# Rotary embedding in f32: one in-order SP queue of 2 MB transfers, and six of 32 tiles summed on TensorE

## The chip, the core and the metric

The kernel runs on one core of a Trainium2 chip. The engines that matter: VectorE (DVE in the profile), GpSimd (POOL), ScalarE (ACT), TensorE (PE), and SyncE (SP), which computes nothing and issues DMA transfers. The transfers of every queue are carried out by the same 16 DMA engines of the core. The metric is device time in microseconds of the slowest (here the only) core, lower is better.

## The reference: what is computed

```python
x1 = x[..., : x.shape[-1] // 2]
x2 = x[..., x.shape[-1] // 2 :]
cos = cos[None, :, None, :]
sin = sin[None, :, None, :]
out1 = x1 * cos - x2 * sin
out2 = x1 * sin + x2 * cos
return np.concatenate([out1, out2], axis=-1)
```

`x` is 8 x 2048 x 8 x 64 in f32 (batch, position, head, feature), 33.55 MB; `cos` and `sin` are 2048 x 32, 0.26 MB each. The output has the shape of `x`. So every byte of `x` is read once and written once, and each element takes part in two multiplications and one addition.

## The kernel before

The 2048 positions are spread over 128 partitions, 16 consecutive positions (R) per partition. A row of one partition and one batch is therefore 16 x 512 f32, 32 KB, contiguous in memory. The kernel cuts it into four pieces of four positions (SL = 4): a tile is 128 partitions x 2048 elements, 1 MB, and there are 32 tiles, ordered by piece and then by batch.

- **Loads** (L55) go through the SP queue, all 32 in a loop ahead of the computation. The pool `xpool` has 20 buffers, so loads from the 21st on wait for a store to release a buffer.
- **Tables**: sine and cosine are loaded through the ACT queue (L48, L49). VectorE writes a negated and a plain copy of the sine side by side into `ssin` (L58, L59), and copies the cosine to PSUM (L60).
- **Per tile**: GpSimd multiplies the swapped halves by the signed sine into `t2`, one instruction per half (L73, two per tile; `t2_pool` has three buffers). VectorE multiplies the tile by the cosine into `t1`, which lies in PSUM (L78, one buffer), and adds `t1` and `t2` back into the tile (L83). The tile is stored through the ACT queue (L84).

Each engine works through its own stream in order. VectorE alternates L78 and L83 of one tile after the other; GpSimd may be ahead of it by as many tiles as `t2` has buffers. ScalarE does no arithmetic, its queue issues the two table loads and the 32 stores; TensorE is not used. In the tables of the profile `t` stands for the `t1` and `t2` buffers.

Of the kernel before, what the change touches and what calls it, by code (L numbers as in the profile page):

```python
# [2 lines left out]

# [4 lines left out]


@with_exitstack  # L10
def kernel(
    ctx: ExitStack,
    tc: tile.TileContext,
    x: bass.AP,
    cos: bass.AP,
    sin: bass.AP,
    out: bass.AP,
):
    nc = tc.nc
    f32 = mybir.dt.float32  # L20

    B, S, H, D = x.shape
    Dh = D // 2
    P = 128
    HD = H * D
    R = S // P

    SL = 4
    n_blk = R // SL
    FREE = SL * HD  # L30

    xv = x.rearrange("b (q r) h d -> b q (r h d)", q=P)
    ov = out.rearrange("b (q r) h d -> b q (r h d)", q=P)
    cos_src = cos.rearrange("(q r) d -> q r d", q=P)
    sin_src = sin.rearrange("(q r) d -> q r d", q=P)

    const_pool = ctx.enter_context(tc.tile_pool(name="const", bufs=1))
    cps_pool = ctx.enter_context(tc.tile_pool(name="cps", bufs=1, space=bass.MemoryType.PSUM))
    t1_pool = ctx.enter_context(tc.tile_pool(name="t1p", bufs=1, space=bass.MemoryType.PSUM))
    xpool = ctx.enter_context(tc.tile_pool(name="xpool", bufs=20))  # L40
    t2_pool = ctx.enter_context(tc.tile_pool(name="t2p", bufs=3))

    cos_sb = const_pool.tile([P, R, Dh], f32, tag="cb")
    sin_sb = const_pool.tile([P, R, Dh], f32, tag="sb")
    ssin = const_pool.tile([P, R, 2, Dh], f32, tag="ss")
    cos_ps = cps_pool.tile([P, R, Dh], f32, tag="cp")

    nc.scalar.dma_start(out=sin_sb, in_=sin_src)  # L48
    nc.scalar.dma_start(out=cos_sb, in_=cos_src)  # L49

    tiles = [(b, l) for l in range(n_blk) for b in range(B)]
    xts = []
    for i, (b, l) in enumerate(tiles):
        xt = xpool.tile([P, FREE], f32, tag="xt", name=f"xt{i}")
        nc.sync.dma_start(out=xt, in_=xv[b, :, l * FREE : (l + 1) * FREE])  # L55
        xts.append(xt)

    nc.vector.tensor_scalar_mul(ssin[:, :, 0, :], sin_sb, -1.0)  # L58
    nc.vector.tensor_copy(ssin[:, :, 1, :], sin_sb)  # L59
    nc.vector.tensor_copy(cos_ps, cos_sb)  # L60

    def rep(a, n):
        return dataclasses.replace(a, ap=[a.ap[0][:], a.ap[1][:], [0, n], a.ap[-1][:]])

    for i, (b, l) in enumerate(tiles):
        xt = xts[i]
        t1 = t1_pool.tile([P, FREE], f32, tag="t1")
        t2 = t2_pool.tile([P, FREE], f32, tag="t2")

        for u in range(2):  # L70
            dst = t2.rearrange("p (rh u d) -> p rh u d", u=2, d=Dh)[:, :, u, :]
            src = xt.rearrange("p (rh u d) -> p rh u d", u=2, d=Dh)[:, :, 1 - u, :]
            nc.gpsimd.tensor_mul(  # L73
                out=dst.rearrange("p (r h) d -> p r h d", h=H),
                in0=src.rearrange("p (r h) d -> p r h d", h=H),
                in1=rep(ssin[:, l * SL : (l + 1) * SL, u, :], H),
            )
        nc.vector.tensor_mul(  # L78
            out=t1.rearrange("p (r k d) -> p r k d", r=SL, d=Dh),
            in0=xt.rearrange("p (r k d) -> p r k d", r=SL, d=Dh),  # L80
            in1=rep(cos_ps[:, l * SL : (l + 1) * SL, :], 2 * H),
        )
        nc.vector.tensor_add(out=xt, in0=t1, in1=t2)  # L83
        nc.scalar.dma_start(out=ov[b, :, l * FREE : (l + 1) * FREE], in_=xt)  # L84


# [1 line left out]
_INS = ['x', 'cos', 'sin']  # L88
_OUTS = [((8, 2048, 8, 64), 'float32')]


# [23 lines left out]
```

## Time and profile before

| | us |
|---|---|
| median of 9 runs (lowest to highest) | 168.26 (168.09 to 168.49) |
| the profiled execution: its time | 168.36 |
| the profiled execution: span from first to last instruction | 166.6 |
| VectorE busy, 67 instructions | 148.2 (89% of the span) |
| GpSimd busy, 68 instructions | 146.3 (88%) |
| DMA: SP queue, share of 16 engines over the span | 48.5% (33.56 MB) |
| DMA: ACT queue, share of 16 engines over the span | 48.6% (34.08 MB) |

The time of the profiled execution is 1.8 us longer than its span, as the span begins with the first instruction and ends with the last. A sum made from durations of the profile is made against the span.

The profile tells where instructions wait, too. These are the waits of SP's queue, in total time, number and longest:

```profile
SPq L55 <- DMA xt<-in_x_dram: 60.2, 13, 8.9
SPq L55 <- DMA out_dram<-xt: 34.8, 6, 13.1
```

A load is issued only once an earlier transfer has landed: at first an earlier load, since a limited number of transfers is under way at once, and later a store that releases the buffer. A wait of this kind stands in the queue, so whatever is behind it in the same queue is not issued either. The page gives the transfers themselves as follows (number, size, median time from issue to landing):

```profile
xt<-in_x_dram SPq DMA_DIRECT2D x32, 1024.0 KB, 20.8
out_dram<-xt ACTq DMA_DIRECT2D x32, 1024.0 KB, 11.4
sin_sb<-in_sin_dram ACTq DMA_DIRECT2D x1, 256.0 KB, 6.0
cos_sb<-in_cos_dram ACTq DMA_DIRECT2D x1, 256.0 KB, 8.7
```

### The profile page before, as it was taken

Reading aid. Unit: us, or ns where it says so; the run is one execution under the profiler, and the core shown is the slowest. Engines: PE = TensorE matmul, PEld = TensorE weight load, DVE = VectorE, ACT = ScalarE, POOL = GpSimd, SP = SyncE. Lnnn points to the kernel's source line nnn. Section 1 sums busy time; section 2 is a strip of 40 time slices with the busy share of each in tenths; the row PEclk is TensorE's granted clock in tenths of the full one; section 3 lists DMA queues with packets and bytes.
Section 4 is the critical chain, followed back from the end, with each engine's and each line's share of the span. In section 5 each row is a group of like instructions: output and inputs, shape, how many; then the busy total and the mean of one; then the engine's idle time right before and its main releaser. Section 6 shows DMA issues by size and latency. Waiting matters only on the chain.

```text
span 166.6 us, 381 instructions
## 1 busy us (share of the span) xinstructions
DVE 148.2 (89%) x67; POOL 146.3 (88%) x68
## 2 busy tenths in 40 slices
DVE  0169999999999999999999999999999999999980
POOL 0299999999999999999999999999999999998000
DMA  5999999999999999999999999999999999999656
GB/s 167 426 426 421 372 423 431 427 425 433 417 439 421 431 429 421 433 421 431 425 425 431 419 437 421 429 431 423 433 419 435 425 427 429 423 435 423 293 220 252
DMA packets 9506, 67.65 MB, mean 406 GB/s; under 512 B 1056, under 2 KB 1056, under 8 KB 1312
## 3 DMA queue, kind: packets, MB, share of 16 engines
q10 hardware_dynamic: 4896, 34.08, 48.6%
q1 hardware_dynamic: 4608, 33.56, 48.5%
q14 instruction: 2, 0.02, 0.0%
HBM read 34.08 MB, written 33.55 MB: 406 GB/s over the span
## 4 chain that ended last, share of the span: by engine, by line
DVE 89%; DMA 5%; issue 2%; DVEq 0%; ACTq 0%
DVE t L78 44%; DVE xt L83 44%; DMA cos_sb<-in_cos_dram 5%; DVE cos_ps L60 0%; DVEq L83 0%; ACTq L48 0%
## 5 line engine op out<-in xcount | busy, mean ns | idle before, releaser
L73 POOL TENSOR_TENSOR t<-xt,ssin 128x1024 f32<-128x1024 f32 x64 | 146.1, 2337 | 6.8 <-DVE ssin L58 6.8
L83 DVE TENSOR_TENSOR xt<-t,t 128x2048 f32<-128x2048 f32 x32 | 73.3, 2292 | 3.3
L78 DVE TENSOR_TENSOR t<-xt,cos_ps 128x2048 f32<-128x2048 f32 x32 | 73.4, 2295 | 1.1
L58 DVE TENSOR_SCALAR ssin<-sin_sb 128x512 f32<-128x512 f32 x1 | 0.4, 428 | 6.8 <-DMA sin_sb<-in_sin_dram 6.8
L60 DVE COPY cos_ps<-cos_sb 128x512 f32<-128x512 f32 x1 | 0.7, 696 | 2.4 <-DMA cos_sb<-in_cos_dram 2.4
L59 DVE COPY ssin<-sin_sb 128x512 f32<-128x512 f32 x1 | 0.4, 420 | 0.0
L99 POOL MEMSET const-float32-0.0<- 128x1 f32 x1 | 0.1, 98 | 0.2 <-issue 0.2
L99 POOL MEMSET const-bfloat16-1.0<- 128x1 bf16 x1 | 0.1, 101 | 0.0
L99 POOL MEMSET const-uint8-127<- 128x1 uint8 x1 | 0.1, 101 | 0.0
L99 POOL MEMSET const-float32-1.0<- 128x1 f32 x1 | 0.1, 98 | 0.0
## 6 DMA issues: line engine op xcount, KB each, us to landing
xt<-in_x_dram SPq DMA_DIRECT2D x32, 1024.0 KB, 20.8
out_dram<-xt ACTq DMA_DIRECT2D x32, 1024.0 KB, 11.4
sin_sb<-in_sin_dram ACTq DMA_DIRECT2D x1, 256.0 KB, 6.0
cos_sb<-in_cos_dram ACTq DMA_DIRECT2D x1, 256.0 KB, 8.7
```

The costliest lines, as they stand in the source:

```text
L58: nc.vector.tensor_scalar_mul(ssin[:, :, 0, :], sin_sb, -1.0)
L59: nc.vector.tensor_copy(ssin[:, :, 1, :], sin_sb)
L60: nc.vector.tensor_copy(cos_ps, cos_sb)
L73: nc.gpsimd.tensor_mul(out=dst.rearrange("p (r h) d -> p r h d", h=H), in0=src.rearrange("p (r h) d -> p r h d", h=H), in1=rep(ssin[:, l * ...
L78: nc.vector.tensor_mul(out=t1.rearrange("p (r k d) -> p r k d", r=SL, d=Dh), in0=xt.rearrange("p (r k d) -> p r k d", r=SL, d=Dh), in1=rep ...
L83: nc.vector.tensor_add(out=xt, in0=t1, in1=t2)
L99: nc = _bacc.Bacc("TRN2", target_bir_lowering=False, num_devices=1)
```

## The change

Four things change together.

1. **Slabs in one queue.** The unit of transfer is a slab of eight positions (SL = 8, 128 x 4096 elements, 2 MB); there are 16 slabs and nine buffers. Loads and stores are both issued by SP, in program order: the sine table, nine slab loads, and then, slab by slab, the store of slab i followed by the load of slab i + 8 into the buffer of slab i - 1. Only the cosine table is loaded through the ACT queue.
2. **Small first and last pieces.** Slab 0 is loaded and computed in pieces of 1, 1, 2 and 4 positions (256 KB, 256 KB, 512 KB, 1 MB); the last slab is computed and stored in pieces of 4, 2, 1 and 1. All others are loaded and stored whole and computed in two units of four positions, each as large as a tile before.
3. **Six units on TensorE.** Slabs 3, 7 and 11 have a first unit of kind C and a second unit of kind B. In B, GpSimd multiplies by the sine and VectorE by the cosine, as before, but both products lie in SBUF; TensorE multiplies each by the identity and accumulates both in PSUM, 512 columns at a time, and ScalarE copies the sum into the slab. In C, VectorE makes both products (two multiplications, neither with swapped halves), and TensorE does the swap and the sign by its choice of columns and by a negated identity; GpSimd has no part. The other 26 unit-sized parts (kind A) are computed as before.
4. **Tables.** GpSimd builds an identity matrix; ScalarE negates the identity and the sine and copies the sine to PSUM; VectorE copies the cosine to PSUM. For kind A and B, GpSimd now does the half with the plain sine first and the half with the negated sine second.

```diff
--- before.py
+++ after.py
@@ -18,6 +18,7 @@
 ):
     nc = tc.nc
     f32 = mybir.dt.float32
+    PSUM = bass.MemoryType.PSUM
 
     B, S, H, D = x.shape
     Dh = D // 2
@@ -25,9 +26,12 @@
     HD = H * D
     R = S // P
 
-    SL = 4
-    n_blk = R // SL
-    FREE = SL * HD
+    SL = 8
+    n_half = R // SL
+    SLAB = SL * HD
+    UNIT = 4 * HD
+    NBUF = 9
+    C = 512
 
     xv = x.rearrange("b (q r) h d -> b q (r h d)", q=P)
     ov = out.rearrange("b (q r) h d -> b q (r h d)", q=P)
@@ -35,53 +39,153 @@
     sin_src = sin.rearrange("(q r) d -> q r d", q=P)
 
     const_pool = ctx.enter_context(tc.tile_pool(name="const", bufs=1))
-    cps_pool = ctx.enter_context(tc.tile_pool(name="cps", bufs=1, space=bass.MemoryType.PSUM))
-    t1_pool = ctx.enter_context(tc.tile_pool(name="t1p", bufs=1, space=bass.MemoryType.PSUM))
-    xpool = ctx.enter_context(tc.tile_pool(name="xpool", bufs=20))
+    tab_pool = ctx.enter_context(tc.tile_pool(name="tab", bufs=1, space=PSUM))
+    t1_pool = ctx.enter_context(tc.tile_pool(name="t1p", bufs=1, space=PSUM))
+    o_pool = ctx.enter_context(tc.tile_pool(name="op", bufs=2, space=PSUM))
+    t1s_pool = ctx.enter_context(tc.tile_pool(name="t1s", bufs=3))
+    xpool = ctx.enter_context(tc.tile_pool(name="xpool", bufs=NBUF))
     t2_pool = ctx.enter_context(tc.tile_pool(name="t2p", bufs=3))
 
     cos_sb = const_pool.tile([P, R, Dh], f32, tag="cb")
     sin_sb = const_pool.tile([P, R, Dh], f32, tag="sb")
-    ssin = const_pool.tile([P, R, 2, Dh], f32, tag="ss")
-    cos_ps = cps_pool.tile([P, R, Dh], f32, tag="cp")
-
-    nc.scalar.dma_start(out=sin_sb, in_=sin_src)
+    nsin = const_pool.tile([P, R, Dh], f32, tag="ns")
+    eye = const_pool.tile([P, P], f32, tag="eye")
+    neye = const_pool.tile([P, P], f32, tag="neye")
+    cos_ps = tab_pool.tile([P, R, Dh], f32, tag="cp")
+    sin_ps = tab_pool.tile([P, R, Dh], f32, tag="sp")
+
+    slabs = [(b, l) for l in range(n_half) for b in range(B)]
+    last = len(slabs) - 1
+    xts = {}
+
+    def cuts(i):
+        if i == 0:
+            return [HD, HD, 2 * HD, UNIT]
+        return [SLAB]
+
+    def pieces(i):
+        if i == 0:
+            return [HD, HD, 2 * HD, UNIT]
+        if i == last:
+            return [UNIT, 2 * HD, HD, HD]
+        return [UNIT, UNIT]
+
+    def stores(i):
+        return pieces(i) if i == last else [SLAB]
+
+    def spans(sizes):
+        lo = 0
+        for n in sizes:
+            yield lo, n
+            lo += n
+
+    def load(i):
+        b, l = slabs[i]
+        xt = xpool.tile([P, SLAB], f32, tag="xt", name=f"xt{i}")
+        for lo, n in spans(cuts(i)):
+            nc.sync.dma_start(
+                out=xt[:, lo : lo + n],
+                in_=xv[b, :, l * SLAB + lo : l * SLAB + lo + n],
+            )
+        xts[i] = xt
+
+    nc.sync.dma_start(out=sin_sb, in_=sin_src)
     nc.scalar.dma_start(out=cos_sb, in_=cos_src)
-
-    tiles = [(b, l) for l in range(n_blk) for b in range(B)]
-    xts = []
-    for i, (b, l) in enumerate(tiles):
-        xt = xpool.tile([P, FREE], f32, tag="xt", name=f"xt{i}")
-        nc.sync.dma_start(out=xt, in_=xv[b, :, l * FREE : (l + 1) * FREE])
-        xts.append(xt)
-
-    nc.vector.tensor_scalar_mul(ssin[:, :, 0, :], sin_sb, -1.0)
-    nc.vector.tensor_copy(ssin[:, :, 1, :], sin_sb)
+    for i in range(NBUF):
+        load(i)
+
+    nc.gpsimd.memset(eye, 0.0)
+    nc.gpsimd.affine_select(
+        out=eye,
+        in_=eye,
+        compare_op=mybir.AluOpType.not_equal,
+        fill=1.0,
+        base=0,
+        pattern=[[-1, P]],
+        channel_multiplier=1,
+    )
+    nc.scalar.mul(nsin, sin_sb, -1.0)
+    nc.scalar.mul(neye, eye, -1.0)
     nc.vector.tensor_copy(cos_ps, cos_sb)
+    nc.scalar.copy(sin_ps, sin_sb)
 
     def rep(a, n):
         return dataclasses.replace(a, ap=[a.ap[0][:], a.ap[1][:], [0, n], a.ap[-1][:]])
 
-    for i, (b, l) in enumerate(tiles):
-        xt = xts[i]
-        t1 = t1_pool.tile([P, FREE], f32, tag="t1")
-        t2 = t2_pool.tile([P, FREE], f32, tag="t2")
-
-        for u in range(2):
-            dst = t2.rearrange("p (rh u d) -> p rh u d", u=2, d=Dh)[:, :, u, :]
-            src = xt.rearrange("p (rh u d) -> p rh u d", u=2, d=Dh)[:, :, 1 - u, :]
-            nc.gpsimd.tensor_mul(
-                out=dst.rearrange("p (r h) d -> p r h d", h=H),
-                in0=src.rearrange("p (r h) d -> p r h d", h=H),
-                in1=rep(ssin[:, l * SL : (l + 1) * SL, u, :], H),
+    kinds = {}
+    for i in (3, 7, 11):
+        kinds |= {(i, 0): "C", (i, UNIT): "B"}
+
+    def rotate(i, lo, n):
+        b, l = slabs[i]
+        kind = kinds.get((i, lo), "A")
+        xt = xts[i][:, lo : lo + n]
+        r0 = l * SL + lo // HD
+        nr = n // HD
+        xk = xt.rearrange("p (r k d) -> p r k d", r=nr, d=Dh)
+        xu = xt.rearrange("p (g u d) -> p g u d", u=2, d=Dh)
+        if kind == "A":
+            t1 = t1_pool.tile([P, n], f32, tag="t1")
+        else:
+            t1 = t1s_pool.tile([P, n], f32, tag="t1s")
+        if kind == "C":
+            t2 = t1s_pool.tile([P, n], f32, tag="t1s")
+        else:
+            t2 = t2_pool.tile([P, n], f32, tag="t2")
+        t1u = t1.rearrange("p (g u d) -> p g u d", u=2, d=Dh)
+        t2u = t2.rearrange("p (g u d) -> p g u d", u=2, d=Dh)
+        if kind != "C":
+            for u, tab in ((1, sin_sb), (0, nsin)):
+                nc.gpsimd.tensor_mul(
+                    out=t2u[:, :, u, :].rearrange("p (r h) d -> p r h d", h=H),
+                    in0=xu[:, :, 1 - u, :].rearrange("p (r h) d -> p r h d", h=H),
+                    in1=rep(tab[:, r0 : r0 + nr, :], H),
+                )
+        nc.vector.tensor_mul(
+            out=t1.rearrange("p (r k d) -> p r k d", r=nr, d=Dh),
+            in0=xk,
+            in1=rep(cos_ps[:, r0 : r0 + nr, :], 2 * H),
+        )
+        if kind == "A":
+            nc.vector.tensor_add(out=xt, in0=t1, in1=t2)
+        elif kind == "B":
+            for j in range(n // C):
+                o = o_pool.tile([P, C], f32, tag="o")
+                cs = slice(j * C, (j + 1) * C)
+                nc.tensor.matmul(o, eye, t1[:, cs], start=True, stop=False)
+                nc.tensor.matmul(o, eye, t2[:, cs], start=False, stop=True)
+                nc.scalar.copy(xt[:, cs], o)
+        else:
+            nc.vector.tensor_mul(
+                out=t2.rearrange("p (r k d) -> p r k d", r=nr, d=Dh),
+                in0=xk,
+                in1=rep(sin_ps[:, r0 : r0 + nr, :], 2 * H),
             )
-        nc.vector.tensor_mul(
-            out=t1.rearrange("p (r k d) -> p r k d", r=SL, d=Dh),
-            in0=xt.rearrange("p (r k d) -> p r k d", r=SL, d=Dh),
-            in1=rep(cos_ps[:, l * SL : (l + 1) * SL, :], 2 * H),
-        )
-        nc.vector.tensor_add(out=xt, in0=t1, in1=t2)
-        nc.scalar.dma_start(out=ov[b, :, l * FREE : (l + 1) * FREE], in_=xt)
+            G = C // Dh
+            for u in range(2):
+                for j in range(n // 2 // C):
+                    o = o_pool.tile([P, C], f32, tag="o")
+                    gs = slice(j * G, (j + 1) * G)
+                    nc.tensor.matmul(o, eye, t1u[:, gs, u, :], start=True, stop=False)
+                    nc.tensor.matmul(
+                        o, eye if u else neye, t2u[:, gs, 1 - u, :], start=False, stop=True
+                    )
+                    nc.scalar.copy(xu[:, gs, u, :], o.rearrange("p (g d) -> p g d", d=Dh))
+
+    for i, (b, l) in enumerate(slabs):
+        done = 0
+        st = list(spans(stores(i)))
+        for lo, n in spans(pieces(i)):
+            rotate(i, lo, n)
+            done = lo + n
+            while st and st[0][0] + st[0][1] <= done:
+                slo, sn = st.pop(0)
+                nc.sync.dma_start(
+                    out=ov[b, :, l * SLAB + slo : l * SLAB + slo + sn],
+                    in_=xts[i][:, slo : slo + sn],
+                )
+        if i >= 1 and i - 1 + NBUF <= last:
+            load(i - 1 + NBUF)
```

## The prediction

> **What bounds the kernel now.** I read the page from the DMA rows to the chain of waits, and then the table of stretches.
>
> ```profile
> DMA  5999999999999999999999999999999999999656
> GB/s 167 426 426 421 372 423 431 427 425 433 417 439 421 431 429 421 433 421 431 425 425 431 419 437 421 429 431 423 433 419 435 425 427 429 423 435 423 293 220 252
> ...
> DVE 89%; DMA 5%; issue 2%; DVEq 0%; ACTq 0%
> ```
>
> The chain that ended last is VectorE, a multiply (44%) and an add (44%) per tile, so at first sight VectorE is the bound. The two rows above say that the DMA engines are full too: one rate of about 427 GB/s from the second slice to the 37th, whether they load, mix or store. Only the first slice and the last three fall. Both resources are nearly equal: 32 tiles at 4.72 us (the chain starts a multiply at 10.65, 15.37, 20.10) are 151.2 us of VectorE, and 67.65 MB at 427 GB/s are 158.4 us of DMA.
>
> ```profile
> L73 POOL TENSOR_TENSOR t<-xt,ssin 128x1024 f32<-128x1024 f32 x64 | 146.1, 2337 | 6.8 <-DVE ssin L58 6.8
> L83 DVE TENSOR_TENSOR xt<-t,t 128x2048 f32<-128x2048 f32 x32 | 73.3, 2292 | 3.3
> L78 DVE TENSOR_TENSOR t<-xt,cos_ps 128x2048 f32<-128x2048 f32 x32 | 73.4, 2295 | 1.1
> ```
>
> These are the costliest groups: POOL is 146.1/32 = 4.57 us per tile, just under VectorE. What the change can win lies where DMA is not full; the table of stretches (columns: length, VectorE busy, POOL busy, clock, DMA share, GB/s) has it:
>
> ```profile
> 15.00:17.50 2.50, 2.47 (x2) 2.50 (x2) 1.00 1.02 426
> 17.50:20.00 2.50, 2.40 (x2) 2.50 (x2) 1.00 1.01 341
> 20.00:21.00 1.00, 0.96 (x2) 1.00 (x1) 1.00 0.96 393
> 21.00:142.00 121.00, 117.45 (x52) 121.00 (x55) 1.00 1.01 427
> 142.00:156.50 14.50, 14.09 (x7) 11.40 (x5) 1.00 1.01 426
> 156.50:158.00 1.50, 1.47 (x2) 0.00 (x0) 1.00 0.21 87
> 158.00:160.50 2.50, 2.40 (x2) 0.00 (x0) 1.00 0.96 397
> 160.50:162.50 2.00, 1.31 (x1) 0.00 (x0) 1.00 0.00 0
> 162.50:165.20 2.70, 0.00 (x0) 0.00 (x0) 1.00 0.94 388
> ```
>
> At 156.5 the backlog of stores is gone and DMA waits for VectorE's last two tiles, then for the last 1 MB. Loss against 427 GB/s: 340/427 x 1.5 = 1.19, 30/427 x 2.5 = 0.18, 2.0, and 39/427 x 2.7 = 0.25: together **3.6 us**. The only other loss after the start is 0.50 + 0.08 = 0.58 us at 17.5 to 21, when the first store joins the loads.
>
> **VectorE and POOL.** Of 32 tile-sized units, 26 keep multiply and add (26 x 4.72 = 122.8); three (B) keep the multiply, now written to SBUF (3 x 2.36 = 7.1; the add that writes SBUF takes 2292 ns against 2295, so the place costs nothing); three (C) take two multiplies on VectorE (3 x 4.72 = 14.2). The first and last slab are cut in four instead of two: eight more VectorE instructions. A 512-wide one takes 696 ns (the cos_ps copy), a 2048-wide one 2292; the line through both leaves 0.16 us fixed, with the gap 0.22 us, so 1.75 us. With the cos_ps copy, 0.72: 146.6 us against 151.9. POOL does 29 units, 29 x 4.57 = 132.4 us; the identity matrix is built there while the sine table is under way (POOL idles 6.8 us at that point).
>
> **The start.** Sine lands at 6.76 and cosine at 9.9 because both share the engines with 1 MB loads and sit in one queue. After, 0.5 MB of tables comes first, side by side on two queues; about 0.64 MB has moved by 4.0 us in the trace. I estimate that VectorE starts at 5.5 us instead of 9.9. If ScalarE prepares its function before it issues the cosine transfer, that slips by up to 2.7 us (the Trainium skill, "ScalarE: Activation LUTs", What ACT_TABLE_LOAD costs; the trace has no ScalarE work). VectorE then ends at 5.5 + 146.6 = 152.1 (bounds 151 to 155) instead of 161.8. This does not count by itself: it becomes **cover of about 8 us**.
>
> **The DMA queue.** Bytes and the 427 GB/s stay. All stores and slab loads now issue from SP in order; ACT keeps only the cosine load. A 2 MB slab takes 2.097/427 = 4.91 us. Nine loads fill the queue till 2.5 + 0.5/0.427 + 9 x 4.91, about 48 us. Then the order is S0 S1 L9 S2 L10 S3. L9 waits on SP for S0 to land, and S2 stands behind it; but S1 is already queued, 4.91 us of work, while a landing and a new issue cost about 2.5 us (the last store takes 3.9 us from issue to landing, of which 2.45 move bytes; a load's first bytes come about 1 us after issue). From L10 on two transfers cover each wait. At most eight transfers are in flight by the waits of the SP queue (loads on the sine table and on earlier loads); with 2 MB that is no limit. Each store waits for its slab in order. Tightest of the offloaded ones: S11 has 16 loads and 11 stores ahead, so its turn is at 137 us; VectorE passes C of slab 11 at 111, and the TensorE tail below ends at 125 at full clock, 139 at half. S15, the last, starts at 157; VectorE ends at 152. So after the change the late thing is DMA alone.
>
> **Small pieces, rule against row.** The Trainium skill ("DMA: Bandwidth & Descriptors", Rules for kernel authors and Measured) wants at least 1 MiB per DMA and gives each about 2.0 us of fixed cost; that speaks against six more, 256 to 512 KB pieces: up to 12 us if each paid. The row says otherwise for queued ones: 1 MB transfers ran at 426, though by its table 1 MB would do 341, and the two 256 KB tables did not break the rate of 4 to 10 us. I take nothing for queued pieces; one landing at the very end is paid before too (1.4 us from last byte to end of span).
>
> **Directions in one queue.** The unknown that decides. Loads alone in the SP queue ran at 426 (15.0 to 17.5), stores alone in the ACT queue at 426 (142 to 156.5, after the last load landed near 138). One queue that turns from loads to stores is not in the trace. The nearest row is the first store's 0.58 us. The Trainium skill ("DMA: Bandwidth & Descriptors", Two DMAs through the same engine are not ordered) says that descriptors of a queue start in order but overlap, the read and write sides apart: by it a turn costs nothing. There are 15 turns (8 to stores, 7 to loads), of which one loss is already in the span. By the rule 0; by the row 14 x 0.58 = 8.1 us. I take the rule's end, since in 21 to 142 the engines alternate directions packet by packet at 427; both ends stay for the range. Below zero: at most the 0.58 us, if that loss came from two queues.
>
> **TensorE and ScalarE.** No row shows either. Each offloaded unit has 8 matmuls of 128x512 in f32: the skill ("FP8 and Floating Point Precision", TensorE Precision Notes) counts four passes, so an estimate of 4 x 512/2.4 GHz = 0.85 us each, or 1.7 at the cold half clock ("TensorE: Matmul & The Clock Gate", Part 1), 13.7 to 27.3 us per slab. ScalarE's 24 evacuations of 128x512 I take as the 696 ns copy, 17 us in all. Both lie beside VectorE with a slab of time to spare. They matter where they hold a buffer: B's t2, one of three, which POOL wants back.
>
> **Sum.** 166.6 - 3.6 = 163.0 us of span; the profiled run has 168.36 - 166.6 = 1.76 around it: 164.8. The shown median is 0.1 below the profiled run: **164.6 us**. Cross-check: 2.5 + 158.4 + 0.6 + 1.4 = 162.9. Its own range: 164.0 (0.58 gained) to 166.5 (0.13 us per turn).
>
> **Rivals.** *A, turns cost (0.22).* Place: each change of direction in the SP queue; price 0.25 us or more. For: the first store's 0.58 us, in which loads slowed. Against: the full rate of the mixed stretch. At 0.58 for turns to stores alone: +4.1, 168.7 us; for all: 172.7. It decides from 3.6/14 = 0.26 us per turn; beyond, slower than before.
>
> *B, the t2 buffer (0.13).* After C and B come units that need t2; with strict rotation the third takes B's. VectorE wants its sum 2.36 + 9.45 + 2.36 = 14.2 us after C; POOL needs 4.57, so TensorE must be through in 9.6 us. At full clock it is 4.1 us late, three times 12.3: VectorE ends at 164.4, the last 256 KB needs some 3.0 more (4.8 for 1 MB in the trace, less 0.75 MB of bytes): span 167.4, 169.1 us. At half clock far more, about 210. It decides from 2.7 us per slab. Against: the buffers freed by VectorE in between can be handed out first, and then nothing waits.
>
> *C, the tail is not filled (0.03).* SP's wait for landings leaves holes and the old loss returns: 168.2, no change.
>
> **Chances.** 0.62 for the forecast. Faster by over 0.2% (0.34 us, about what this measurement can tell) 0.63, with cheap turns of A; within 0.2%: 0.04; slower: 0.33. The range takes A up to full price on turns to stores and B at full clock: 163.9 to 170.0.
>
> **What would show it.** Right: DMA near 427 GB/s till 161 us, no hole at 48 to 60 us, VectorE done near 152 with the chain ending in SP's stores. Wrong: dips each 5 us from 48 to 120 us at full DMA share (A); POOL idle behind TensorE in slabs 4, 8 and 12 and VectorE ending after 160 (B); SP waits with an idle DMA (C).

## The result, and the profile after

The changed kernel takes 166.71 us (median of 10 runs, 165.92 to 167.23) against 168.31 us (30 runs): a ratio of 0.990, 95% interval 0.989 to 0.991. It is faster, as forecast, but by 1.6 us where 3.7 were forecast. The profiled execution took 165.92 us, the shortest of the ten, with a span of 164.1 us. Times are medians over a kernel's executions; one of the twelve of the alternating halves below, 180.45 us, is left out as a slow one.

The page of the changed kernel, rows of busy time, of slices and of the chain of waits:

```profile
PE 53.5 (33%) x96; PEld 21.3 (13%) x96; DVE 140.6 (86%) x70; ACT 16.7 (10%) x28; POOL 134.9 (82%) x72
...
GB/s 150 427 445 443 407 427 447 427 403 447 443 395 435 447 419 419 435 433 423 419 435 433 403 439 419 443 423 431 415 439 427 435 427 439 423 435 427 423 404 67
...
DVE 52%; POOL 26%; issue 11%; DMA 2%; DVEq 0%; SPq 0%; POOLq 0%
```

VectorE has 140.6 us of work in place of 148.2, and the DMA engines stay full to the last slice but one; the fall of the last three slices (293, 220, 252) is gone. The chain adds up to 91% only: it is followed back from VectorE's last instruction, which ends at 151.65 us. The 12.4 us after it are no engine's, they are the queue of stores. That stretch by itself (columns: length; PE, PEld, VectorE, ScalarE, POOL busy; clock; DMA share; GB/s):

```profile
159.00:160.00 1.00, 0.00 (x0) 0.00 (x0) 0.00 (x0) 0.00 (x0) 0.00 (x0) 0.50 1.02 399
160.00:160.50 0.50, 0.00 (x0) 0.00 (x0) 0.00 (x0) 0.00 (x0) 0.00 (x0) 0.50 0.84 328
160.50:161.00 0.50, 0.00 (x0) 0.00 (x0) 0.00 (x0) 0.00 (x0) 0.00 (x0) 0.50 0.28 107
161.00:161.50 0.50, 0.00 (x0) 0.00 (x0) 0.00 (x0) 0.00 (x0) 0.00 (x0) 0.50 0.12 49
161.50:162.00 0.50, 0.00 (x0) 0.00 (x0) 0.00 (x0) 0.00 (x0) 0.00 (x0) 0.50 0.13 49
162.00:162.50 0.50, 0.00 (x0) 0.00 (x0) 0.00 (x0) 0.00 (x0) 0.00 (x0) 0.50 0.07 25
162.50:163.00 0.50, 0.00 (x0) 0.00 (x0) 0.00 (x0) 0.00 (x0) 0.00 (x0) 0.50 0.06 25
```

Look at the share, not at the rate alone: 0.12 is two of 16 DMA engines, 0.06 is one. Fourteen engines are done by 161.3 us; the kernel waits two more microseconds for the other two.

The trace says since when. A transfer is spread over the 16 engines, and each of them raises the transfer's semaphore once when its part has landed, so every transfer has 16 landing times. First, median and last of them, in us, and the lag of the last behind the first (computed from those records; L is a load, S a store of a slab, numbered as the slabs; S15d is the last piece of the last slab):

```
       first  median  last   lag
L1      14.2   14.3   14.4   0.20
L8      48.5   48.6   48.8   0.30
S1      58.6   58.7   58.9   0.33
L9      63.1   63.2   63.6   0.50
L10     72.8   73.0   74.1   1.28
L12     92.3   92.7   94.6   2.28
L14    111.8  112.2  114.5   2.80
L15    121.5  121.9  124.3   2.84
S14    155.5  155.9  158.3   2.81
S15d   160.5  160.9  163.3   2.81
```

All 16 engines are abreast here while the queue only loads (in the runs below the lag of the first loads is 0.4 to 1.3 us). From 48 to 122 us, where stores and loads alternate, a few engines fall behind, 2.8 us in the end; in the stores that follow, with the queue full, the lag stays as it is. An average over 16 engines hides this until the end. Where the queues ran dry the lag went: before the change they did at 156.5 and 160.5 us, and the lag fell from 0.91 us in the store before to 0.15 us in the last one.

### The profile page after: what moved, and what is told of

Same layout as the page of the kernel before. It is cut to its first block, busy times and chain, and to the rows that moved or that the text cites. A ratio compares the mean times of both kernels' runs of the same rounds, so it can differ in the third digit from the quotient of the medians.

```text
span 164.1 us, 547 instructions
## 1 busy us (share of the span) xinstructions
PE 53.5 (33%) x96; PEld 21.3 (13%) x96; DVE 140.6 (86%) x70; ACT 16.7 (10%) x28; POOL 134.9 (82%) x72
## 4 chain that ended last, share of the span: by engine, by line
DVE 52%; POOL 26%; issue 11%; DMA 2%; DVEq 0%; SPq 0%; POOLq 0%
POOL t L139 26%; DVE t L144 25%; DVE xt L150 24%; DVE t L159 3%; DMA xt<-in_x_dram 2%; DVEq L150 0%; SPq L92 0%; POOLq L139 0%; DVEq L144 0%
## 5 line engine op out<-in xcount | busy, mean ns | idle before, releaser
L139 POOL TENSOR_TENSOR t<-xt,sin_sb 128x1024 f32<-128x1024 f32 (+2 forms) x33 | 68.8, 2085 | 12.8 <-DVE xt L150 5.3
L144 DVE TENSOR_TENSOR t<-xt,cos_ps 128x2048 f32<-128x2048 f32 (+2 forms) x36 | 73.6, 2055 | 0.9
L139 POOL TENSOR_TENSOR t<-xt,nsin 128x1024 f32<-128x1024 f32 (+2 forms) x33 | 68.8, 2086 | 0.0
L150 DVE TENSOR_TENSOR xt<-t,t 128x2048 f32<-128x2048 f32 (+2 forms) x30 | 60.2, 2007 | 5.6 <-POOL t L139 3.1
L169 PE MATMUL o<-t,eye 128*128 128x512 f32 x24 | 18.6, 886 | 70.0 <-DVE t L144 70.0
L169 PEld LDWEIGHTS o<-t,eye 128*128 128x128 f32 x24 | 6.3, 280 | 78.7 <-issue 77.7
L173 ACT COPY xt<-o 128x512 f32<-128x512 f32 x12 | 7.0, 586 | 92.1 <-PE o L170 92.1
L155 PE MATMUL o<-t,eye 128*128 128x512 f32 x24 | 12.3, 592 | 0.0
L156 PE MATMUL o<-t,eye 128*128 128x512 f32 x24 | 12.3, 592 | 0.0
L170 PE MATMUL o<-t,neye 128*128 128x512 f32 x12 | 10.7, 1025 | 1.3 <-DVE t L159 1.2
L157 ACT COPY xt<-o 128x512 f32<-128x512 f32 x12 | 7.0, 586 | 13.6 <-PE o L156 13.6
L159 DVE TENSOR_TENSOR t<-xt,sin_ps 128x2048 f32<-128x2048 f32 x3 | 6.8, 2278 | 0.0
L170 PE MATMUL o<-t,eye 128*128 128x512 f32 x12 | 6.1, 592 | 0.0
L156 PEld LDWEIGHTS o<-t,eye 128*128 128x128 f32 x24 | 4.6, 190 | 5.7 <-issue 5.7
L155 PEld LDWEIGHTS o<-t,eye 128*128 128x128 f32 x24 | 4.6, 190 | 5.7 <-issue 5.7
L170 PEld LDWEIGHTS o<-t,neye 128*128 128x128 f32 x12 | 3.4, 316 | 9.0 <-issue 5.3
L170 PEld LDWEIGHTS o<-t,eye 128*128 128x128 f32 x12 | 2.4, 202 | 3.4 <-issue 3.4
```

The source lines that it names most:

```text
L139: nc.gpsimd.tensor_mul(out=t2u[:, :, u, :].rearrange("p (r h) d -> p r h d", h=H), in0=xu[:, :, 1 - u, :].rearrange("p (r h) d -> p r h d" ...
L144: nc.vector.tensor_mul(out=t1.rearrange("p (r k d) -> p r k d", r=nr, d=Dh), in0=xk, in1=rep(cos_ps[:, r0 : r0 + nr, :], 2 * H),)
L155: nc.tensor.matmul(o, eye, t1[:, cs], start=True, stop=False)
L156: nc.tensor.matmul(o, eye, t2[:, cs], start=False, stop=True)
L157: nc.scalar.copy(xt[:, cs], o)
L159: nc.vector.tensor_mul(out=t2.rearrange("p (r k d) -> p r k d", r=nr, d=Dh), in0=xk, in1=rep(sin_ps[:, r0 : r0 + nr, :], 2 * H),)
```

## The experiments

Each lag below is read from the one traced execution of its kernel; how much it varies from one execution to the next was not seen.

Two theories of the lag at first. TURNS: the single queue turns from loads to stores and back, and some engines lose time at a turn. OFFLOAD: the lag grew mostly at 70 to 90 and 107 to 125 us, when TensorE and ScalarE worked, so their traffic slows some DMA engines. A third, MIX, came with the second run: loads and stores under way together, in whatever queue.

**All units of kind A** (e1), so no TensorE and no evacuation:

```diff
-    for i in (3, 7, 11):
+    for i in ():
```

> All 16 slabs are of kind A: no unit is summed on TensorE, ScalarE evacuates nothing; queue, slab size and pieces as in the changed kernel. In the changed kernel the 16 DMA engines land together (spread 0.2 us) until 48 us and then drift apart while loads and stores alternate: the last store lands on its first engine at 160.6 and on its last at 163.4, a lag of 2.8 us. Theory TURNS (an engine loses time when its one queue turns between loads and stores): the lag stays, 2 to 3 us at 125 us. Theory OFFLOAD (the lag grew in the stretches 70-90 and 107-125 us in which TensorE and ScalarE worked, so their traffic delays some DMA engines): the lag at 125 us is under 0.9 us. Time: VectorE ends near 159 (151.65 plus 7.1 of adds less small waits), so 164.5 to 165.5 under OFFLOAD and 166.5 to 167.5 under TURNS.

Measured: the lag is 0.5 us at S1 and 3.2 us at L15, as large as with TensorE at work. The time is 166.18 us (166.16 to 166.50), ratio 0.987 (0.986 to 0.989). OFFLOAD falls by the lag; the time lies between the two expectations. Without the six units the kernel is not slower; VectorE ends at 160.1 us, the queue runs short before the last pieces, and the late engines catch up a little (lag 3.0 in the first store of the last slab, 1.9 at the last landing).

**Stores from the ACT queue** (e2), the rest as changed:

```diff
-                nc.sync.dma_start(
+                nc.scalar.dma_start(
                     out=ov[b, :, l * SLAB + slo : l * SLAB + slo + sn],
```

> The changed kernel with its stores issued from the ACT queue, so that loads and stores stand in two queues of the same 16 engines; nothing else is changed, but ScalarE's copies now share a stream with the stores' waits. TURNS: no queue turns, the lag at the last store is under 1 us and the time 163.3 to 164.5 if ScalarE's copies are not held up. OFFLOAD: the lag of 2 to 3 us stays, 166 to 167.5. A third theory, MIX (loads and stores under way together make some engines slower, by whatever queue), also says that the lag stays.

Measured: 165.12 us (164.77 to 165.27), ratio 0.981 (0.979 to 0.983), and a lag of 1.03 us at the last store. So MIX does not explain the 2.8 us: both directions are under way for most of the time, and what is left at the end is 1.0. The time is a little above the expected 164.5. Two queues are not free of lag, though. Lags in us of four kernels with loads in one queue and stores in the other: of the last load before the first store, and the largest ones after it (e4 and e11 follow below):

```
                          first    beside each other   stores alone,
                          loads    loads    stores     queue full
kernel before, 1 MB       0.83     2.15     1.65       1.03
stores from ACT (e2)      0.50     1.80     1.12       1.14
DMA alone (e4)            0.61     1.49     0.55       0.87
all of kind A (e11)       1.29     2.84     1.10       1.34
```

While both queues are served, each moves at half the pace (loads of 2 MB land 9.7 us apart in e2, 4.9 in one queue), so an engine with the same work left shows about twice the lag. That would explain why the 2.8 us of e11 do not reach the end; it is an inference, as the landings do not say which engine they belong to.

**DMA alone, one queue (e3) and two (e4).** The call that does a unit's arithmetic is left out, so that slabs are only loaded and stored; in the second kernel stores go through the ACT queue.

```diff
         for lo, n in spans(pieces(i)):
-            rotate(i, lo, n)
             done = lo + n
```

> All arithmetic on x is left out: each slab is loaded and stored unchanged, in the order and pieces of the changed kernel on the one SP queue. TURNS: the lag of 2 to 3 us is there without any engine at work, time 165.5 to 166.5. OFFLOAD: all engines land within 0.5 us, time 163 to 163.8. MIX: as TURNS.

> As the run with one queue and no arithmetic, but with stores issued from the ACT queue. TURNS: lag under 1 us, time 163 to 163.8, 2 us below the run with one queue. MIX: lag of 2 us or more as with one queue. OFFLOAD: both runs alike, without lag.

Measured: 166.78 us (166.54 to 167.03) with one queue, 164.48 us (164.34 to 164.62) with two, which is 0.7 us above what was expected; lags of 3.15 and 0.86 us. The ends of the two in the table of stretches (no PE columns here: VectorE, ScalarE, POOL). One queue:

```profile
160.00:160.50 0.50, 0.00 (x0) 0.00 (x0) 0.00 (x0) 1.00 1.02 401
160.50:161.00 0.50, 0.00 (x0) 0.00 (x0) 0.00 (x0) 1.00 0.24 90
161.00:161.50 0.50, 0.00 (x0) 0.00 (x0) 0.00 (x0) 1.00 0.12 49
161.50:162.00 0.50, 0.00 (x0) 0.00 (x0) 0.00 (x0) 1.00 0.14 57
162.00:162.50 0.50, 0.00 (x0) 0.00 (x0) 0.00 (x0) 1.00 0.12 45
162.50:163.00 0.50, 0.00 (x0) 0.00 (x0) 0.00 (x0) 1.00 0.14 53
163.00:163.50 0.50, 0.00 (x0) 0.00 (x0) 0.00 (x0) 1.00 0.10 37
```

Two queues:

```profile
160.00:160.50 0.50, 0.00 (x0) 0.00 (x0) 0.00 (x0) 1.00 1.08 418
160.50:161.00 0.50, 0.00 (x0) 0.00 (x0) 0.00 (x0) 1.00 0.85 328
161.00:161.50 0.50, 0.00 (x0) 0.00 (x0) 0.00 (x0) 1.00 0.21 78
161.50:162.00 0.50, 0.00 (x0) 0.00 (x0) 0.00 (x0) 1.00 0.00 0
```

With no engine at work the tail of two engines is the same, and the whole kernel is no slower than its transfers alone in that order (166.71 against 166.78). So the time after the change is a DMA time, and 2.3 us of it (166.78 less 164.48) belong to the single alternating queue.

**Fewer turns, and smaller steps.** If turns make the lag, their number should set it. In the full kernel the queue was reordered to nine loads, seven stores, seven loads, nine stores (e5; e7 is its transfers alone, e6 and e6b the transfers alone in steps of 1 MB, a store and a load by turns or two and two):

```diff
-        if i >= 1 and i - 1 + NBUF <= last:
-            load(i - 1 + NBUF)
+        if i == 6:
+            for k in range(NBUF, last + 1):
+                load(k)
```

> The changed kernel in full, its one SP queue reordered: nine loads, then the first seven stores together, then the last seven loads together, then the other stores. The queue turns from stores to loads once instead of seven times. TURNS (lag grows at each turn from stores to loads): the last store's 16 landings are within 1.0 us of each other instead of 2.8, span about 162, time 163.3 to 164.5. MIX or total bytes per engine: the lag of 2 to 3 us stays and the time is 166 to 167. Should a slab arrive late for VectorE, the time is longer in both; by the sums slab 9 lands at 87 us and is wanted at 89.

> All arithmetic on x is left out (slabs are loaded and stored unchanged); one SP queue with one turn from stores to loads. TURNS: lag 0.5 to 1.2 us, time 163.5 to 164.5, against 3.2 us and 166.8 with seven turns. MIX: lag 2 to 3 us.

> All arithmetic on x is left out; one SP queue, transfers of 1 MB, a store and a load alternating by halves of a slab: about 14 turns from stores to loads instead of 7. TURNS: the lag about doubles, to 5 to 7 us, time 169 to 170.5. If the lag belongs to the bytes moved while both directions are under way, it stays near 3.2 us and the time near 166.8.

> As the run with alternating halves, with the same 1 MB transfers, but two stores and two loads at a time, so 7 turns from stores to loads as in the 2 MB run. TURNS: lag 3 to 3.5 us and 166.5 to 167 us as with 2 MB. If the size of a transfer makes the lag, it follows the alternating halves.

Measured: the reordered kernel takes 164.76 us (164.53 to 165.14), ratio 0.980 (0.978 to 0.981), with a lag of 1.4 us, of which 0.9 to 1.0 were there in the first loads: 2 us less than the changed kernel, but time and lag are both a little above what was expected. Its transfers alone take 163.98 us with a lag of 0.55. The halves contradict the count of turns. Alternating 1 MB stores and loads, with twice the turns, left a lag of 0.95 us instead of 5 to 7; paired, with the old number of turns, it was 2.95, in 167.89 us, 0.9 more than expected. The alternating run took 167.60 us all the same, and its page says where:

```profile
GB/s 150 391 426 428 426 422 424 422 420 424 420 424 428 353 319 434 422 434 422 434 422 424 432 424 432 424 432 424 432 424 432 424 432 424 432 422 434 422 424 222
```

In the slices with 353 and 319, at its first turns, all engines slowed together. That could have levelled them, so the test was repeated with one more half store ahead of the first load (e8), and a middle point was added (e9): two stores and two loads of 2 MB by turns (only its last turn, the store of slab 7 and the load of slab 15, is of single slabs).

> All arithmetic on x is left out. As the run with alternating halves (1 MB stores and loads by turns, 14 turns each way), but four half stores lead instead of three, to see whether the slow stretch at that run's first turns (353 and 319 GB/s) goes and whether its small lag (0.95 us) was owed to that stretch. TURNS by number: lag 5 to 7 us, time 169 to 170.5. If alternating in 1 MB steps makes no lag: lag under 1.2 us and, without the slow stretch, 165.7 to 166.5.

> All arithmetic on x is left out. One SP queue, 2 MB transfers, two stores and two loads at a time: four turns each way in place of eight to stores and seven to loads. If each turn at 2 MB or more costs some engines alike, the lag is about half of 3.2 us, 1.3 to 2.0, and the time 165.0 to 165.8, between three turns (163.98) and fifteen (166.78). If the lag is made only by the strict alternation of single slabs, it is under 0.8 us and the time 164 to 164.5.

Measured, transfers alone (lag at the end of the first loads and at the last store; slow packets are full-size packets of the queues after 30 us that took over 1.1 times the usual one, 0.61 us for 16 KB and 0.31 for 8 KB):

```
order in the queue                          lag, us        slow packets   time, us
one queue, 14 MB by turns (e7)              0.41 -> 0.55    1             163.98
one queue, 4 MB by turns (e9)               0.86 -> 2.58   29             165.87
one queue, 2 MB by turns (e3)               0.79 -> 3.15   22             166.78
one queue, 2 MB by turns, 1 MB each (e6b)   0.74 -> 2.95   22             167.89
one queue, 1 MB by turns, late (e8)         0.62 -> 0.70    2             166.07
one queue, 1 MB by turns (e6)               0.64 -> 0.95    82            167.60
two queues, 2 MB each (e4)                  0.61 -> 0.86    0             164.48
```

The slow stretch did not come back in the repeat, and again strict 1 MB alternation made no lag. So the number of turns does not set the lag: long stretches and 1 MB stretches make hardly any, and 2 to 4 MB stretches in one queue do. The contrasts hold within one chip each: e7 against e6b, e8 against e9, e4 against e3. Little lag is not yet little time: e8 still takes 2.1 us more than e7, as its engines all come in late (the median one lands at 162.6 us against 160.9).

In the run at 2 MB (e3), 22 of the 3297 full-size packets after 30 us are slow; they took up to 1.32 us and exceed the usual time by 5.9 us in sum. Over the same stretch the lag of the other 15 engines behind the first, added up, grew by 4.8 us (3.75 to 8.5), so these packets are enough to make it; in the changed kernel it is 45 packets, 8.7 and 8.3 us. The trace does not say which engine a packet belongs to, so that the slow ones are those of the late engines is not shown. In e3 each of them begins in the last 2.9 us before the median landing of a load slab, ahead of the store behind it; for none of them is the next landing a store's. Why a few engines are hit there, and only with stretches of this length, stays open; no run changed what the engines find in their queues without changing the order.

**One part alone: a small end in the kernel before (e10).** VectorE does the last tile of the old kernel in pieces of 2, 1 and 1 positions, each stored at once:

```diff
+        for r0, nr in ((0, 2), (2, 1), (3, 1)) if i == len(tiles) - 1 else ((0, SL),):
...
-        nc.scalar.dma_start(out=ov[b, :, l * FREE : (l + 1) * FREE], in_=xt)
+            nc.scalar.dma_start(
+                out=ov[b, :, l * FREE + r0 * HD : l * FREE + (r0 + nr) * HD], in_=xt[:, cs]
+            )
```

> The kernel before, with one part of the change alone: VectorE computes its last tile in pieces of 2, 1 and 1 positions, each stored at once (512, 256 and 256 KB). VectorE gets four more instructions (0.9 us), and the last store is 256 KB in place of 1 MB, whose bytes take 1.8 us less. So 0.9 us less than before: 167.2 to 167.5. If the end is set by a fixed cost of the last transfer, no change.

Measured: 167.62 us (167.43 to 167.76) against 168.29, ratio 0.996 (0.995 to 0.997): 0.7 us, 0.2 less than the sum.

**Two queues, all units of kind A** (e11, the edits of e1 and e2 together):

> The changed kernel with stores issued from the ACT queue and no unit on TensorE (all of kind A). Against the run with stores on ACT and six units on TensorE (165.12) this shows what these units are worth when no engine lags. By VectorE's sum it ends near 159.5 and the last 256 KB lands 3 us later: span 162.5 to 163.5, time 164.3 to 165.3, so within 0.5 us of the run with TensorE. If VectorE's relief is needed for the DMA engines to stay full to the end, 166 or more.

Measured: 165.01 us (164.68 to 165.10), ratio 0.980 (0.979 to 0.982); with the six units on TensorE it was 165.12 (ratio 0.981). They are worth nothing here. The table of stretches for this kernel says why the two meet:

```profile
158.00:160.00 2.00, 1.76 (x4) 0.00 (x0) 0.00 (x0) 1.00 0.95 386
160.00:161.00 1.00, 0.35 (x1) 0.00 (x0) 0.00 (x0) 1.00 0.53 201
161.00:162.00 1.00, 0.00 (x0) 0.00 (x0) 0.00 (x0) 1.00 0.70 264
```

VectorE works to 160.35 us and the last 256 KB are out by 162.4. VectorE's small pieces and the DMA engines run out almost together, so there is little that relieving VectorE further could still save.

## Why the prediction was right and wrong

- **VectorE's work and the start: right.** Forecast 152.1 us for its end, measured 151.65; it started at 4.55 us where 5.5 was estimated, and needed 147.1 from there where the sum was 146.6. Sine landed at 4.3 and cosine at 4.5 us. ScalarE's function load (1.28 us, at 1.16) came after the cosine's issue (at 0.73) and did not delay it, so that bound was not needed.
- **VectorE leaves the critical path: right.** The changed kernel takes as long as its transfers alone. That its relief by TensorE is worth anything, no run shows: without the six units the kernel takes 166.18 us in one queue and 165.01 in two, no more than with them.
- **SP's waits: right.** From 48 to 160 us the DMA engines never ran dry; the stretches read (PE, PEld, VectorE, ScalarE, POOL busy, clock, DMA share, GB/s):

```profile
48.00:120.00 72.00, 37.50 (x71) 15.01 (x70) 70.33 (x32) 10.25 (x18) 66.80 (x30) 0.72 1.01 429
120.00:160.00 40.00, 4.83 (x12) 1.84 (x10) 29.61 (x17) 2.06 (x4) 24.90 (x15) 0.59 1.00 427
```

- **Small pieces: right by the row, not by the rule.** The last two 256 KB stores landed 0.63 us apart at the median engine (160.27 and 160.90), which is their bytes at about 416 GB/s; the fixed 2.0 us that the formula of the Trainium skill ("DMA: Bandwidth & Descriptors", Anatomy of one DMA) adds to each transfer is not to be seen in a full queue. The page fits it to transfers issued from GpSimd, and measured its 341 GB/s on such; the prediction did not say that these here are issued from SP and ACT.
- **Rival B: as good as absent, for the reason that the prediction had put against it.** The waits (engine, line, releaser: total, times, longest) hold one such event, at 125 us:

```profile
POOL t L139 <- PE o L156: 3.5, 1, 3.5
DVE xt L150 <- POOL t L139: 3.1, 4, 1.1
```

  TensorE itself was as slow as estimated. The program has 12 matmuls on L155 and the page has 24: each stands in the trace as two records. Two rows of the timeline in slab 3 (start, length):

```profile
L155 PE MATMUL o<-t,eye 128*128 128x512 f32 x24 | 12.3, 592 | 0.0
48.13 1.02 PE L155 MATMUL o<-t,eye 128*128 128x512 f32 x2
48.98 1.02 PE L156 MATMUL o<-t,eye 128*128 128x512 f32 x2
```

  So a matmul takes 0.86 us at full clock (estimate 0.85), and 1.7 in the first ones of a slab, whose records start 0.85 us apart. TensorE read B's buffer of slab 3 until 55.2 us. With strict rotation POOL would have wanted it for the third unit after B's; it started that unit at 47.29, on the buffer that VectorE's add had just freed (at 47.21). In slab 7 it was the same (81.91 after 81.83, B's being read until 89.5). Only in slab 11 did POOL come back to B's buffer too early, and VectorE lost 1.1 us by it.
- **A term missing, 1.2 us to the good.** The sum kept 427 GB/s for 2 MB transfers. The forecast span of 163.0 puts the last landing at 162.1 (the end came 0.87 us after the last landing before the change); the median engine landed at 160.9. Larger transfers are worth most of it: with the same turns, the transfers alone in 1 MB steps (e6b) brought the median engine in at 161.9, in 2 MB steps (e3) at 160.9 (one trace each).
- **The step that failed: "Directions in one queue", "by it a turn costs nothing ... I take the rule's end".** The term was put at 0, and the single queue that turns between directions cost 2.4 us, from 160.9 (median engine) to 163.3 (last). With the two terms, both read off the landings, the sum closes as it must: 162.1 - 1.2 + 2.4 = 163.3, the measured last landing; the span is then 164.1 instead of 163.0, and the profiled run 165.9 instead of 164.8. The other 0.8 us to the median of the ten runs are in executions without a trace; their spans go to 165.4, and whether they hold a larger lag was not seen.
- **Rival A had the place and not the form.** It priced a turn for all engines alike and asked for dips in the rate. There are none: fourteen engines lose little (0.8 us at most), and two lose 1.9 and 2.8 us, which no average shows. Nor does the price follow the number of turns, as A had it. The rule of the Trainium skill on ordering ("DMA: Bandwidth & Descriptors", Two DMAs through the same engine are not ordered: descriptors start in order and overlap) speaks of one queue on one engine, and of the 16 engines it says only that nothing orders DMAs across them; that a turn is free was my inference from it. The mixed stretch of the old trace, my second ground, was of two queues, and its mean rate of 427 GB/s could not show the engines apart: there too the loads' landings were up to 2.15 us from first to last.

With the turns taken out, by two queues (165.12) or by the reordered queue (164.76), the kernel comes to about 0.5 us or less from the forecast of 164.6. That is in part luck: a rate a little better than forecast makes up for the lag that is left (1.0 and 1.4 us). These versions, and two queues without TensorE (165.01), are faster than both kernels; among the three the intervals overlap.

## What to carry to other kernels

When a kernel is bound by its transfers, the end is set by the slowest of the 16 DMA engines: read the landings of the first and the last engine, or DMA shares of one or two sixteenths at the end, before trusting a mean rate. In a queue that stayed full no late engine caught up (2.8 us from 122 us to the end). Here stores and loads by turns of 2 to 4 MB in one queue cost 2 to 3 us; two queues, or longer stretches of one direction, avoided most of it, and shaving an engine that had cover gave nothing.

## What had not been expected of the hardware

- Lag does not follow the number of turns: 14 turns each way at 1 MB left 0.70 us, seven to loads at 2 MB 3.15 us, four at 4 MB (the last of them of single slabs) 2.58 us.
- Very few packets are slow, and they are enough for the lag: 22 of 3297 (e3), up to 1.32 us instead of 0.61.
- A lag goes when the queue runs short: in e11 it was 1.34 us in the stores of a full queue and 0.16 us in the last one.
- Loads of 2 MB in one queue landed 4.89 us apart on the changed kernel's first engine (429 GB/s); in transfers alone the stretch from 10 to 48 us ran at 424 GB/s with 1 MB (e8) and at 431 with 2 MB (e3).
- At the first turns of the alternating run all engines slowed together (353 and 319 GB/s, over 8 us), and with one more half store ahead of them they did not.
